# A hybrid GLA and RG-LRU layer on one core: the last modulation block on the vector engine, the gate row in a context bank

## The chip, the cores and the metric

The kernel runs on one core of a Trainium2 chip, in float32. The metric is the device time of one execution in microseconds (us). The engines are TensorE (PE; its weight loads are listed as PEld), VectorE (DVE), ScalarE (ACT), GpSimd (POOL) and SyncE (SP). Transfers that move data from and to HBM are issued by SP and by POOL.

## The reference

One layer with `D_MODEL` 2048, 512 latent tokens and 256 context tokens:

```python
mod_x = silu(c) @ w_ada + b_ada              # 3 x 2048: shift, scale, gate
mod_c = silu(c_ctx) @ w_ada + b_ada          # the same weights for the context
hn    = rmsnorm(h, g_norm) * (1 + scale) + shift
parts = split(hn @ w_in)                     # q, k, v, gates, recurrent input, merge gates
...                                          # gated linear attention and RG-LRU, both directions
x     = x + gate * merge_out(...)
out   = rmsnorm(x, g_final)
```

What matters here is the modulation: the products of two vectors (s = 0 for the latent tokens, s = 1 for the context) with the shift and scale columns of `w_ada`, 33.5 MB, and with its gate columns for s = 0 alone.

## The kernel before

Features stand on the partitions, in 16 groups of 128 called k. Every float32 operand of a large product is split into a rounded part (hi) and a rest (lo), ScalarE making hi and VectorE lo, and a product is three matmuls. The time from the beginning to about 206 us is written by `start` (L465). It has these streams of work:

- *Tokens.* Eight tiles `tok0` to `tok7` (two k each) are loaded, squared and summed for the norm; `tok8` to `tok11` (context) come later in the same way.
- *Modulation.* The shift and scale columns come as 64 pieces of 512 KB, cut into blocks (L43): blocks 0 to 3 hold one k and four pieces each, blocks 4 to 9 hold two k and eight pieces. `ada` (L676) multiplies the pieces of a block into PSUM tile `pa`, 32 rows wide (the two vectors and zeros), two pieces a call in blocks of two k. After the last piece of a block ScalarE copies `pa` out, `mod` (L701) transposes it into `pm` and builds the factors `AB`, and `modulate` (L725) makes xhi and xlo of each k: VectorE, ScalarE, VectorE (L731, L733, L735).
- *Key projection.* `key` (L832) works through a strict list (L748 to L754): first for every k the six column tiles of the latent keys (PSUM tiles `kx`), three items of two tiles for each k up to 13 and, for k = 14 and 15 together, six items of one tile and both k. An item is six matmuls of 512 columns. A second phase has the context keys (`kc`) and the two column tiles left over. The key weights come on POOL's queue as `kraw`, and `ksplit` (L783) splits them; those of k are asked for when those of k - 2 are split, and split when k - 3 is used up.

A planner in the code orders all this. It holds one clock per engine, an estimate of each transfer's landing (`fetch`, L481) and due times, and writes the instructions in the order in which its clocks reach them; on the chip each engine then runs its list in order. When key weights and the modulated k are ready it alternates between `ada` and key items. VectorE's and ScalarE's work stands in `todo` (done as soon as it is ready) and `idle` (when both engines have nothing planned).

Pieces land in buffers called slots: four tiles `araw0` to `araw3`, then `tok8` to `tok11` as long as they are not needed for the context (pieces from 24 on may not use them, L644), and from tok1 on each `tok` tile once both of its k are modulated (L742). `loads` (L640) issues the transfers in the fixed order `order` (L632) and stops at the first one for which no slot is free.

After the start the kernel runs a list of weight pieces through `run`. Side work is put between its matmuls: recurrent blocks (`rnn_block`, L983), whose products `rx` and `rc` use PSUM tags sa and sb with one bank each, and `gate_row` (L1073). The gate columns of the modulation are multiplied and added by VectorE into `gacc` (L1063 to L1067); for each half of the columns `gate_row` then sums over the partitions with two matmuls (L1079) into `pr`, tag sa, copies each row out (`grow`) and stores it. The tag pc has two banks, for the context accumulators of the projections that have any.

Of the kernel before, what the change touches and what calls it, by code (L numbers as in the profile page):

```python
# [5 lines left out]
F32 = mybir.dt.float32  # L6
F32R = mybir.dt.float32r
AF = mybir.ActivationFunctionType
ALU = mybir.AluOpType
# [3 lines left out]
P = 128  # L13
# [41 lines left out]
class Kern:  # L55
# [409 lines left out]
    def start(self, sp, raw0, raw, prime):  # L465
# [46 lines left out]
        hot = []  # L512
# [8 lines left out]
        def poll():  # L521
            n = 0
            while n < len(todo):
                if todo[n][0]() <= T["pe"]:
                    todo.pop(n)[1]()
                    n = 0
                else:
                    n += 1
            while max(T["dve"], T["act"]) <= T["pe"] + LAG:
                ok = [i for i in idle if i[0]() <= T["pe"]]  # L530
                if not ok:
                    break
                idle.remove(ok[0])
                ok[0][1]()
            loads()
# [90 lines left out]
        blocks = START_BLOCKS  # L626
        pieces = [(b, i) for b, ks in enumerate(blocks) for i in range(4 * len(ks))]

        slots = [(0.0, raw0.tile([P, 1024], F32, name=f"araw{i}")) for i in range(4)] + [(0.0, t) for t in tok[8:12]]
        araw = {}  # L630
        nada, nload = [0], [0]
        order = [("tok", i) for i in range(8)]  # L632
        for n in range(len(pieces)):
            order.append(("ada", n))
            if n in (3, 7):
                order.append(("key", 0))
            elif n in (31, 35, 39, 43):
                order.append(("tok", 8 + (n - 31) // 4))

        def loads():  # L640
            while nload[0] < len(order):
                kind, n = order[nload[0]]
                if kind == "ada":
                    f = [s for s in slots if n < 24 or all(s[1] is not t for t in tok[8:12])]  # L644
                    if not f:
                        return
                    slots.remove(f[0])
                    d, t = f[0]
                    araw[n] = t, fetch(t, a["wss"][n], dep=d)
                elif kind == "tok":  # L650
                    d = 0.0
                    if n >= 8:
                        f = [s for s in slots if s[1] is tok[n]]
                        if not f or px_done[0] < 2:
                            return
                        slots.remove(f[0])
                        d = f[0][0]
                    load_tok(n, d)
                else:
                    load_key(nc.sync)  # L660
                nload[0] += 1
# [2 lines left out]

        def ada_ready():
            n = nada[0]
            if n >= len(pieces):
                return INF
            b, i = pieces[n]

            w = n + len(blocks[b]) - 1
            if w not in araw:
                return INF
            return max(araw[w][1], pa_free[0] if i == 0 else 0.0)

        def ada():  # L676
# [18 lines left out]
            if i == 4 * m - 1:  # L695
# [2 lines left out]
                r = pa_free[0] = at("act", w / 1200 + 0.18, T["pe"] + 0.3)  # L698
                hot.append((lambda: max(r, sb_free[0]), lambda: mod(b, row, r)))

        def mod(b, row, r):  # L701
            m = len(blocks[b])
            pm = self.ps.tile([P, 2 * m, 4, 32], F32, tag="sb", name="pm")
            for j in range(2 * m):
                nc.tensor.transpose(pm[:, j, :, :].rearrange("p q c -> p (q c)"), row[:, j * P:(j + 1) * P], self.ident)
            t = pe("pm", 0.22 * m, r, sb_free[0])
            ms = sp.tile([P, 4, 4, 2], F32, tag="ms", name="ms")
            m4 = sp.tile([P, 4, 2, 2], F32, tag="m4", name="m4")
            m2 = sp.tile([P, 4, 2], F32, tag="m2", name="m2")
            v = nc.vector  # L710
            nc.scalar.activation(out=ms[:, 0:2 * m], in_=pm[:, :, :, 0:2], func=AF.Copy)
            t = sb_free[0] = at("act", 0.2, t + 0.2)
            v.tensor_tensor(out=m4[:, 0:2 * m], in0=ms[:, 0:2 * m, 0:2, :], in1=ms[:, 0:2 * m, 2:4, :], op=ALU.add)
            v.tensor_tensor(out=m2[:, 0:2 * m], in0=m4[:, 0:2 * m, 0, :], in1=m4[:, 0:2 * m, 1, :], op=ALU.add)
            for kk, k in enumerate(blocks[b]):
                v.tensor_scalar(out=AB[:, k, 0, :], in0=m2[:, kk, :], scalar1=sc1[:, k:k + 1],
                                scalar2=par[:, PC_GN + k:PC_GN + k + 1], op0=ALU.add, op1=ALU.mult)
                v.tensor_scalar(out=AB[:, k, 1, :], in0=m2[:, m + kk, :], scalar1=par[:, PC_SH + k:PC_SH + k + 1],
                                scalar2=None, op0=ALU.add)
            r = at("dve", 0.4 + 0.42 * m, t)  # L720
            for s in range(2):
                for k in blocks[b]:
                    (idle if s else todo).append((lambda s=s: max(r, tok_ok[s]), lambda k=k, s=s: modulate(k, s, r)))

        def modulate(k, s, r):  # L725
            hi, lo = ((self.xhi, self.xlo), (self.chi, self.clo))[s]
            w = width[s]
            n = 1024 // w
            x = tok[8 * s + k // n][:, k % n * w:k % n * w + w]
            m, b = AB[:, k, 0, s:s + 1], AB[:, k, 1, s:s + 1]  # L730
            nc.vector.scalar_tensor_tensor(out=x, in0=x, scalar=m, in1=rms[s], op0=ALU.mult, op1=ALU.mult)  # L731
            t = at("dve", w / 960 + 0.22, r, tok_ok[s])
            nc.scalar.activation(out=hi[:, k, :], in_=x, func=AF.Identity, bias=b)  # L733
            t = at("act", w / 1200 + 0.3, t)
            nc.vector.scalar_tensor_tensor(out=lo[:, k, :], in0=x, scalar=b, in1=hi[:, k, :].bitcast(F32), op0=ALU.add,  # L735
                                           op1=ALU.subtract)
            rk[k, s] = t = at("dve", w / 960 + 0.22, t)
            if s == 0:
                px_done[k // 2] += 1
                if px_done[k // 2] == 2 and k > 1:  # L740

                    slots.append((t, tok[k // 2]))  # L742
# [40 lines left out]
        def ksplit(n):  # L783
            t, r = kraw.pop(n)
            hi = self.ring.tile([P, 1024], F32R, tag="whi", name="khi")
            lo = self.ring.tile([P, 1024], F32R, tag="wlo", name="klo")
            w = cols[n // KT] // 2
            for u in (slice(0, w), slice(w, 2 * w)):
                nc.scalar.activation(out=hi[:, u], in_=t[:, u], func=AF.Copy)
                e = at("act", w / 1200 + 0.2, r)  # L790
                nc.vector.tensor_tensor(out=lo[:, u], in0=t[:, u], in1=hi[:, u].bitcast(F32), op=ALU.subtract)
                e = at("dve", w / 960 + 0.16, e)
            wk[n // KT, n % KT] = hi, lo, e
            kfree[n % 2] = e
            load_key(nc.gpsimd)
            ksplit_soon()
# [64 lines left out]

        loads()
        primed = None
        while nada[0] < len(pieces) or hot or fifo:
            poll()
            cand = []
            now = T["pe"]
            if hot:
                cand.append((hot[0][0](), 0))
            kr = key_ready()  # L870
            cand.append((kr, 2))

            if not (fifo and kr <= now and last[0] != "pa" and fifo[0][2][0] != ("x", 0)
                    and rk.get((fifo[0][1][-1] + 1, 0), INF) <= now):
                cand.append((ada_ready(), 1))
            t0 = max(now, min(c[0] for c in cand))
            pend = [t[0]() for t in todo] + [max(t[0](), T["dve"] - LAG, T["act"] - LAG) for t in idle]
            if t0 > now and pend and min(pend) < t0 and min(pend) > now:
                T["pe"] = min(pend)
                continue  # L880
            assert t0 < INF, (now, cand, pend, len(fifo))
            which = min((p for r, p in cand if r <= t0))
            if which == 0:
                hot.pop(0)[1]()
            elif which == 1:
                ada()
            else:
                key()
            if primed is None and nksplit[0] == 2 * KT and not kraw:
                primed = prime()  # L890
            if primed and len(fifo) <= 3:
                primed()
                primed = False
        for t in todo + idle:
            t[1]()

# [176 lines left out]
    def gate_row(self, acc, hf):  # L1073
        nc = self.nc
        for j in range(2):
            row = self.rp.tile([P, 512], F32, tag="grow", name="grow")[0:1]
            yield self.dep(acc)
            pr = self.ps.tile([1, 512], F32, tag="sa", name="pr")
            nc.tensor.matmul(pr, lhsT=self.ones, rhs=acc[:, j * 512:(j + 1) * 512], start=True, stop=True)  # L1079
            self.act(row, pr)  # L1080
            c0 = hf * 1024 + j * 512
# [623 lines left out]
```

## Time and profile before

| | us |
|---|---|
| median of 3 runs | 2301.71 (2299.45 to 2301.82) |
| the profiled execution | 2301.33 |
| its span | 2299.6 |
| PE, DVE, ACT, POOL busy | 2269.1, 1166.8, 1015.9, 104.6 |
| HBM read and written | 270.69 MB, 30.42 MB |

The span runs from the first to the last instruction; the time of the execution has a little more around it. Busy shares are means over the whole span. In rows, `128x512` is partitions by elements, `x8` a count of instructions. One float32 matmul of `ada`, `mod` and the sums shows as two matmul instructions, so one `ada` call of two pieces is `x8`.

### The profile page before, as it was taken

To read this page: it belongs to the slowest core of one execution; us is meant where nothing else is said; L and a number is where in the kernel's file an instruction comes from. 1 tells how busy PE (TensorE), PEld (TensorE's weight loads), DVE (VectorE), ACT (ScalarE), POOL (GpSimd) and SP (SyncE) were. 2 spreads that over 40 slices of the span, in tenths; PEclk is the share of its full clock that TensorE was granted. 3 is DMA by queue.
4 is the path that set the end of the run, shared out by engine and by line. 5 is a ranking of instruction groups with operands and counts; after the bars stand their busy time and mean duration, and the time that the engine had idled before them with its cause. 6 is when DMAs were issued, how large, how long until landed. Compare 5 with 4: busy or idle time off the path is not lost.

```text
span 2299.6 us, 29276 instructions
## 1 busy us (share of the span) xinstructions
PE 2269.1 (99%) x12032; PEld 1926.0 (84%) x12032; DVE 1166.8 (51%) x1498; ACT 1015.9 (44%) x1334; POOL 104.6 (5%) x201
## 2 busy tenths in 40 slices
PE   7999999999999999999999999999999999999998
PEld 4588889999898988998888888888888888888886
DVE  4563245655556655646637637637634423434435
ACT  3343255454454445546546556555523312222223
POOL 0010000000000000000000000000000000000000
PEclk9999999999999999999999999999999999999999
DMA  9943222333333332233233233323336633343533
GB/s 392 379 165 129 88 83 88 124 123 109 113 106 124 121 118 83 91 121 110 88 115 119 88 105 128 110 78 115 117 112 199 193 122 123 115 124 120 214 101 119
DMA packets 85814, 303.02 MB, mean 132 GB/s; under 512 B 10416, under 2 KB 11568, under 8 KB 84784
## 3 DMA queue, kind: packets, MB, share of 16 engines
q1 hardware_dynamic: 72656, 255.78, 33.1%
q0 software_dynamic: 13024, 45.37, 5.5%
q8 instruction: 94, 1.54, 0.3%
q14 instruction: 40, 0.33, 0.0%
HBM read 270.69 MB, written 30.42 MB: 131 GB/s over the span
## 4 chain that ended last, share of the span: by engine, by line
PE 85%; issue 10%; DMA 2%; ACT 1%; DVE 1%; POOL 0%; SPq 0%; DVEq 0%; POOLq 0%; ACTq 0%
PE px L127 64%; PE pc L127 6%; PE kx L850 4%; PE po L127 3%; PE kc L850 2%; PE rx L127 1%; PE pa L691 1%; PE pd L127 1%; DMA tok<-in_wss 1%; PE pcs L127 1%; PE rc L127 1%; PE pt L1450 0%; DMA tok<-in_xT 0%; POOL vS L936 0%; ACT g L90 0%
## 5 line engine op out<-in xcount | busy, mean ns | idle before, releaser
L94 DVE TENSOR_TENSOR wlo<-raw,whi 128x1024 fp32r<-128x1024 f32 x304 | 374.5, 1232 | 571.9 <-ACT whi L90 569.8
L90 ACT ACTIVATE whi<-raw 128x1024 fp32r<-128x1024 f32 x304 | 321.2, 1057 | 538.8 <-PE px L127 344.1
L127 PE MATMUL px<-xhi,whi 128*128 128x512 f32 x1408 | 551.0, 391 | 0.0
L127 PE MATMUL px<-xlo,whi 128*128 128x512 f32 x1408 | 549.3, 390 | 0.0
L127 PE MATMUL px<-xhi,wlo 128*128 128x512 f32 x1408 | 548.5, 390 | 0.0
L127 PEld LDWEIGHTS px<-xhi,wlo 128*128 128x128 f32 x1408 | 264.5, 188 | 55.6
L127 PEld LDWEIGHTS px<-xhi,whi 128*128 128x128 f32 x1408 | 264.8, 188 | 54.6 <-issue 2.6
L127 PEld LDWEIGHTS px<-xlo,whi 128*128 128x128 f32 x1408 | 264.9, 188 | 50.5
L127 PE MATMUL px<-whi,xlo 128*128 128x256 f32 x512 | 145.0, 283 | 0.0
L127 PE MATMUL px<-whi,xhi 128*128 128x256 f32 x512 | 145.0, 283 | 0.0
L127 PE MATMUL px<-wlo,xhi 128*128 128x256 f32 x512 | 145.0, 283 | 0.0
L90 ACT ACT_TABLE_LOAD x100 | 128.3, 1283 | 1.7
L127 PE MATMUL px<-yhi,whi 128*128 128x512 f32 x256 | 99.7, 389 | 0.0
L127 PE MATMUL px<-whi,mlo 128*128 128x512 f32 x256 | 99.7, 389 | 0.0
L127 PE MATMUL px<-yhi,wlo 128*128 128x512 f32 x256 | 99.7, 389 | 0.0
L127 PE MATMUL px<-olo,whi 128*128 128x512 f32 x256 | 99.7, 389 | 0.0
L127 PE MATMUL px<-ohi,whi 128*128 128x512 f32 x256 | 99.7, 389 | 0.0
L127 PE MATMUL px<-ohi,wlo 128*128 128x512 f32 x256 | 99.7, 389 | 0.0
L127 PE MATMUL px<-ylo,whi 128*128 128x512 f32 x256 | 99.7, 389 | 0.0
L127 PE MATMUL px<-whi,mhi 128*128 128x512 f32 x256 | 99.7, 389 | 0.0
L127 PE MATMUL px<-wlo,mhi 128*128 128x512 f32 x256 | 99.7, 389 | 0.0
L127 PEld LDWEIGHTS px<-wlo,xhi 128*128 128x128 f32 x512 | 98.3, 192 | 0.2
(328 smaller groups left out, 3966.0 us busy)
## 6 DMA issues: line engine op xcount, KB each, us to landing
raw<-in_w SPq DMA_DIRECT2D x304, 512.0 KB, 3.7
araw<-in_wss SPq DMA_DIRECT2D x35, 512.0 KB, 9.7
raw<-in_wgt SPq DMA_DIRECT2D x32, 512.0 KB, 4.3
tok<-in_wss SPq DMA_DIRECT2D x29, 512.0 KB, 9.7
kraw<-in_w POOLq DMA_DIRECT2D x16, 512.0 KB, 3.9
gS<-mst POOLq DMA_DIRECT2D x32, 256.0 KB, 2.5
gst<-gS POOLq DMA_DIRECT2D x32, 256.0 KB, 2.9
vS<-vt POOLq DMA_DIRECT2D x24, 256.0 KB, 2.5
```

Source lines behind the costliest of these rows:

```text
L90: return self.nc.scalar.activation(out=out, in_=in_, func=func, **kw)
L94: return self.nc.vector.tensor_tensor(out=out, in0=in0, in1=in1, op=op)
L127: self.nc.tensor.matmul(out, lhsT=lhsT, rhs=rhs, start=start, stop=stop, skip_group_check=True)
L691: nc.tensor.matmul(self.pa[32 * q:32 * q + 32], lhsT=S[:, k, :], rhs=raw_[:, kk * w:(kk + 1) * w], start=k < 4, stop=k >= KT - 4, skip_gro ...
L850: nc.tensor.matmul(o, lhsT=l[:, w], rhs=x[:, k, :], start=k == 0 and m == 0 and e == 0, stop=k == KT - 1 and m == 2, skip_group_check=True)
```

## The change

In `start`, the 64 pieces stay, but the last block's eight (56 to 63) are not multiplied by TensorE (`npe` is 56). They are loaded behind pieces 18, 22, ... 46. For each of them VectorE multiplies the two k-rows by the two vectors' columns and adds them into `vacc`, four instructions over 512 columns, 32 in all; they are written where the planner finds VectorE and ScalarE idle (`poll`) and between ScalarE's and VectorE's parts of a modulation or of a key split (`fill`). `vsum` then sums over the partitions with eight matmuls against ones and goes on with the factors as before (`factors`, taken out of `mod`). There are three `araw` tiles instead of four. In `gate_row`, `pr` gets a bank of tag pc instead of sa.

```diff
+                    if vq and vq[0][0] <= T["pe"]:
+                        vmul(*vq.pop(0))
+                        continue
...
+        npe = len(pieces) - 4 * len(blocks[-1])
+        vacc = raw0.tile([P, 2, 512], F32, name="vacc")
+        vq = []
+        def fill():
+            if vq and vq[0][0] <= T["dve"]:
+                vmul(*vq.pop(0))
-        slots = [(0.0, raw0.tile([P, 1024], F32, name=f"araw{i}")) for i in range(4)] + [(0.0, t) for t in tok[8:12]]
+        slots = [(0.0, raw0.tile([P, 1024], F32, name=f"araw{i}")) for i in range(3)] + [(0.0, t) for t in tok[8:12]]
-        for n in range(len(pieces)):
+        for n in range(npe):
             order.append(("ada", n))
...
+            if n >= 18 and n % 4 == 2 and npe + (n - 18) // 4 < len(pieces):
+                order.append(("ada", npe + (n - 18) // 4))
...
+        def vmul(r, n, t, kk, s):
+            k = 2 * pieces[n][1] + kk
+            x, o, c = t[:, kk * 512:(kk + 1) * 512], vacc[:, s, :], self.cs[:, s, k:k + 1]
+            if k == 0:
+                nc.vector.tensor_scalar(out=o, in0=x, scalar1=c, scalar2=None, op0=ALU.mult)
+            else:
+                nc.vector.scalar_tensor_tensor(out=o, in0=x, scalar=c, in1=o, op0=ALU.mult, op1=ALU.add)
+            e = at("dve", 0.75, r)
+            if kk and s:
+                slots.append((e, t))
+            voff[0] += 1
+            if voff[0] == 32:
+                hot.append((lambda: max(e, sb_free[0]), lambda: vsum(e)))
+        def vsum(r):
+            b = len(blocks) - 1
+            pm = self.ps.tile([P, 4, 2, 2], F32, tag="sb", name="pm")
+            for j in range(4):
+                for s in range(2):
+                    nc.tensor.matmul(pm[:, j, s, :], lhsT=vacc[:, s, j * P:(j + 1) * P], rhs=ones[:, 0:2],
+                                     start=True, stop=True)
+            t = pe("pm", 2.4, r, sb_free[0])
+            m2 = sp.tile([P, 4, 2], F32, tag="m2", name="m2")
+            nc.scalar.activation(out=m2, in_=pm[:, :, :, 0], func=AF.Copy)
+            t = sb_free[0] = at("act", 0.2, t + 0.2)
+            factors(b, m2, t)
...
             nc.scalar.activation(out=hi[:, k, :], in_=x, func=AF.Identity, bias=b)
+            fill()
...
                 nc.scalar.activation(out=hi[:, u], in_=t[:, u], func=AF.Copy)
+                fill()
...
-            pr = self.ps.tile([1, 512], F32, tag="sa", name="pr")
+            pr = self.pc.tile([P, 512], F32, tag="pc", name="pr")[0:1]
```

## Rows read from the trace of the kernel before

**Rows 1.** The page: busy time by engine, and the chain that ended last, by line.

```profile
...
PE 2269.1 (99%) x12032; PEld 1926.0 (84%) x12032; DVE 1166.8 (51%) x1498; ACT 1015.9 (44%) x1334; POOL 104.6 (5%) x201
...
PE px L127 64%; PE pc L127 6%; PE kx L850 4%; PE po L127 3%; PE kc L850 2%; PE rx L127 1%; PE pa L691 1%; PE pd L127 1%; DMA tok<-in_wss 1%; PE pcs L127 1%; PE rc L127 1%; PE pt L1450 0%; DMA tok<-in_xT 0%; POOL vS L936 0%; ACT g L90 0%
...
```

**Rows 2.** Stretches: length, busy of PE, PEld, DVE, ACT, POOL, PE clock, DMA share, GB/s.

```profile
...
45.00:60.00 15.00, 15.00 (x85) 7.81 (x88) 5.86 (x17) 3.73 (x9) 1.08 (x2) 1.00 0.93 370
60.00:72.00 12.00, 12.00 (x64) 7.35 (x56) 4.13 (x7) 3.70 (x9) 1.07 (x2) 1.00 0.86 314
72.00:119.80 47.80, 44.83 (x237) 23.31 (x237) 28.17 (x71) 18.10 (x39) 3.22 (x6) 1.00 1.02 411
119.80:140.26 20.46, 20.46 (x96) 15.99 (x95) 13.64 (x29) 11.19 (x23) 1.59 (x3) 1.00 0.37 114
140.26:206.00 65.74, 65.74 (x467) 61.92 (x466) 26.80 (x47) 22.91 (x42) 7.40 (x15) 1.00 0.43 139
...
```

**Rows 3.** PE's waits, 29 to 140 us: us in total, times, longest.

```profile
...
PE pa L691 <- DMA araw<-in_wss: 3.0, 5, 1.2
PE pa L691 <- DMA tok<-in_wss: 1.0, 2, 0.8
...
```

**Rows 4.** The chain of waits in the start: start us, us, what.

```profile
...
18.42 1.80 PE pr L585 x8
...
101.54 0.58 PE pr L594 x4
...
105.47 2.74 PE kx L850 x12
...
116.54 2.92 PE pa L691 x24
...
123.41 1.59 PE kx L850 x6
124.99 0.44 PE pm L705 x4
...
```

**Rows 5.** DVE in order of time: start us, us, what [idle before].

```profile
...
76.18 0.75 DVE L735 SCALAR_TENSOR_TENSOR xlo<-tok,AB,xhi 128x512 fp32r<-128x512 f32 x1 [0.79 <-ACT xhi L733]
76.85 0.74 DVE L731 SCALAR_TENSOR_TENSOR tok<-tok,AB,rms 128x512 f32<-128x512 f32 x1
...
92.10 0.75 DVE L735 SCALAR_TENSOR_TENSOR xlo<-tok,AB,xhi 128x512 fp32r<-128x512 f32 x1 [0.79 <-ACT xhi L733]
...
```

**Rows 6.** DVE's groups, 360 to 900 us: busy us, mean ns.

```profile
...
L99 DVE TENSOR_SCALAR gacc<-raw,cs 128x1024 f32<-128x1024 f32 x2 | 1.5, 748 | 0.0
```

**Rows 7.** SP's issues in order of time, and SP's waits, 45 to 72 us.

```profile
...
49.61 9.44 SPq L482 DMA_DIRECT2D araw<-in_wss  x4
63.13 0.33 SPq L482 DMA_DIRECT2D tok<-in_wss  x1
...
SPq L482 <- PE pa L691: 10.3, 3, 3.8
SPq L482 <- DVE xlo L735: 6.1, 2, 4.0
...
```

**Rows 8.** Key weight loads (POOL's queue): issue to landing.

```profile
...
DMA to landing us min/median/max: 3.7/6.0/9.9
```

**Rows 9.** PE in order of time, two instructions.

```profile
...
85.20 0.62 PE L691 MATMUL pa<-tok,S 128*32 128x512 f32 x2
...
140.26 0.28 PE L850 MATMUL kc<-chi,khi 128*128 128x256 f32 x1
...
```

**Rows 10.** All engines in order of time, around the gate rows.

```profile
...
620.61 0.59 ACT L90 ACTIVATE grow<-pr 1x512 f32<-1x512 f32 x1 [3.26 <-DMA rS<-grow]
...
621.25 0.50 PE L127 MATMUL rx<-xh,wh 128*128 128x512 f32 x1 [0.38 <-ACT grow L90]
...
886.12 1.02 PE L1079 MATMUL pr<-gacc,ones 128*1 128x512 f32 x2 [0.79 <-ACT grow L90]
...
```

More of the change, by code (lines that the diff above doesn't have):

```diff
@@ L627, in start @@
         pieces = [(b, i) for b, ks in enumerate(blocks) for i in range(4 * len(ks))]
-        slots = [(0.0, raw0.tile([P, 1024], F32, name=f"araw{i}")) for i in range(4)] + [(0.0, t) for t in tok[8:12]]
+        npe = len(pieces) - 4 * len(blocks[-1])
+        vacc = raw0.tile([P, 2, 512], F32, name="vacc")
+        voff = [0]
+        vq = []
[3 more added lines that the diff above has]
+        slots = [(0.0, raw0.tile([P, 1024], F32, name=f"araw{i}")) for i in range(3)] + [(0.0, t) for t in tok[8:12]]
         araw = {}
@@ L648, in loads @@
                     d, t = f[0]
-                    araw[n] = t, fetch(t, a["wss"][n], dep=d)
+                    r = fetch(t, a["wss"][n], dep=d)
+                    if n < npe:
+                        araw[n] = t, r
+                    else:
+                        for kk in range(2):
+                            for s in range(2):
+                                vq.append((r, n, t, kk, s))
                 elif kind == "tok":
@@ L666, in ada_ready @@
             n = nada[0]
-            if n >= len(pieces):
+            if n >= npe:
                 return INF
@@ L699, in ada @@
                 hot.append((lambda: max(r, sb_free[0]), lambda: mod(b, row, r)))
+        def vmul(r, n, t, kk, s):
[3 more added lines that the diff above has]
+                nc.vector.tensor_scalar(out=o, in0=x, scalar1=c, scalar2=None, op0=ALU.mult)
+            else:
+                nc.vector.scalar_tensor_tensor(out=o, in0=x, scalar=c, in1=o, op0=ALU.mult, op1=ALU.add)
[9 more added lines that the diff above has]
+            for j in range(4):
+                for s in range(2):
+                    nc.tensor.matmul(pm[:, j, s, :], lhsT=vacc[:, s, j * P:(j + 1) * P], rhs=ones[:, 0:2],
[5 more added lines that the diff above has]
+            factors(b, m2, t)
         def mod(b, row, r):
@@ L714, in mod, with factors @@
             v.tensor_tensor(out=m2[:, 0:2 * m], in0=m4[:, 0:2 * m, 0, :], in1=m4[:, 0:2 * m, 1, :], op=ALU.add)
+            at("dve", 0.4, t)
+            factors(b, m2, t)
+        def factors(b, m2, t):
+            m, v = len(blocks[b]), nc.vector
             for kk, k in enumerate(blocks[b]):
@@ L719, in mod @@
                                 scalar2=None, op0=ALU.add)
-            r = at("dve", 0.4 + 0.42 * m, t)
+            r = at("dve", 0.42 * m, t)
             for s in range(2):
@@ L863, in start @@
         primed = None
-        while nada[0] < len(pieces) or hot or fifo:
+        while nada[0] < npe or hot or fifo:
             poll()
@@ L876, in start @@
             t0 = max(now, min(c[0] for c in cand))
-            pend = [t[0]() for t in todo] + [max(t[0](), T["dve"] - LAG, T["act"] - LAG) for t in idle]
+            pend = [t[0]() for t in todo] + [max(v[0], T["dve"] - LAG, T["act"] - LAG) for v in vq[0:1]] + [max(t[0](), T["dve"] - LAG, T["act"] - LAG) for t in idle]
             if t0 > now and pend and min(pend) < t0 and min(pend) > now:
@@ L893, in start @@
                 primed = False
+        assert not vq
         for t in todo + idle:
```

## The prediction

> **What bounds the kernel now.** I read the page first. TensorE is busy 99% of the span and one group of projection matmuls makes up 64% of the chain that ended last [rows 1], so a gain must be TensorE work taken away or a TensorE wait removed. Both edits lie in short stretches. The first is the start, up to the la pieces at about 206 us; I cut it into stretches next [rows 2]. TensorE is packed from 45 to 72 us and from 119.8 us on, and has its gaps in between: 47.80 - 44.83 = 3.0 us from 72 to 119.8. The column of bytes shows a second resource at its limit. The DMA engines move 411 GB/s from 72 to 119.8 and next to none of the start's operands after that, so the last piece of w_ada lands at about L = 119.8 us. Between 45 and 72 they move 370 and 314 GB/s: against 411 that is 15 x 41/411 + 12 x 97/411 = 1.5 + 2.8 = 4.3 us of idle transfer time. The list of waits names what TensorE lacks: pieces of w_ada, 4.0 us in seven waits [rows 3]. So from 72 to 119.8 TensorE (3.0 us short of full) and the transfers (full) are both within a few per cent of being the bound, and that decides what an edit here is worth.
>
> **The change, part by part.**
>
> *TensorE work of the last block.* Block 9 (k = 14, 15; pieces 56 to 63) costs four calls of `ada`. Three of them back to back took 2.92 us [rows 4], so four take 3.9 us. A key item after a call takes 1.59 instead of 2.74/2 = 1.37 us, 0.22 us for each of the two places where calls and items alternate, 0.4 us in all. The four transposes take 0.44 us. Sum removed: 4.7 us. Added: `vsum` with eight matmuls of two columns against a 128x128 operand. Two such took 0.58 us at 101.5 us [rows 4], so eight take 2.3 us; four took 1.80 us at 18.4 us, which gives 3.6 us as the other end. The block ends late, near the first row's time, so I take 2.3. TensorE loses 2.4 us of work (1.1 to 2.4).
>
> *VectorE work.* 32 instructions over 512 columns. 30 have the form of the modulation's own scalar_tensor_tensor, 0.75 us long and 0.67 us from start to start [rows 5]: 20 us. Two are tensor_scalar; one over 1024 columns took 748 ns [rows 6], so 0.4 us each. Together 21 us, set among 5.9 + 4.1 + 28.2 = 38 us of VectorE work in the 75 us from 45 to 119.8 [rows 2], so it fits. `fill` puts one where VectorE waits 0.79 us for ScalarE in the middle of a modulation [rows 5]: 0.67 into 0.79 costs nothing. In a split of key weights the wait is shorter and up to 0.5 us is lost, but those are made up to two k ahead. If a piece lands later than planned, VectorE waits in order with the modulation's second half behind it: 0 to 1.2 us a time, the largest of seven by which TensorE's own pieces came late [rows 3]. I take 0 and keep the cost for the rival.
>
> *Transfers.* Not a byte less is moved. Eight pieces of 0.524 MB, 1.28 us each at 411 GB/s, are put between pieces 18 and 47, so every block from 4 to 8 comes later by the pieces put ahead of it, and the last to land is now block 8 (k = 12, 13). In the old order it was block 9. All else that had landed by L must also land by the new last piece L', except perhaps one load of key weights (0.39 MB, 0.96 us): these are asked for as TensorE uses up earlier k, and TensorE will be later with them; I take off 0.5 us. Hence L' = 119.8 + (i - 4.3) - 0.5, with i the idle transfer time of the new order. Using some of the 4.3 us is the one real gain here.
>
> What is i? The old idle time comes from landing buffers. From 49.6 to 59.05 SP issues only four pieces and the next comes at 63.1, while SP stands waiting for `ada` calls and for modulations to free a buffer [rows 7]. The code says which: pieces from 24 on may not use tok8 to tok11, so they have araw0 to araw3 and tok1. After the change a buffer fewer is there (vacc takes its room), pieces 56 to 63 fall under the same rule from piece 18 on, and each holds its buffer until four VectorE instructions (2.7 us, after a wait for gaps that I put at 2.5) are through. For it, SP has more to issue in that time, and may: piece 56 goes out before 24. A transfer takes at least 3.7 us from issue to landing [rows 8]; with half a piece (0.64 us) of waiting for its pair, one call (1.0 us) and half a key item (0.7 us) a buffer is held 6.0 us, one of VectorE some 9 us, about 6.6 us on the mean. One piece per 1.28 us, beside a key-weight load every four pieces (0.24 us a piece), needs 6.6/1.52 = 4.3 buffers. Four are there until k = 4 and 5 are done near 63 us, five until about 80. So the gap shrinks little: i from 0 (all used) to 8 (nearly twice as much); I take 3.5, near the old row, and L' = 118.5 us.
>
> The Trainium skill ("DMA: Bandwidth & Descriptors", "Anatomy of one DMA — SWDGE (gpsimd) path") gives a transfer some 2.0 us fixed plus its bytes at 436 GB/s, which would be 3.2 us here, below the shortest measured landing of 3.7; by it the need would be 4.0 buffers and i perhaps 3.0, an estimate that moves the end by 0.5 us. The same page's "Specifications" put the limit of HBM for one core at about 358 GB/s; the 411 GB/s of this trace [rows 2] shows that it doesn't bind here, so I give no weight to a stream slower than before.
>
> *From the last landing to the end of the first key phase.* Block 6's last `ada` call began at 85.20 us [rows 9] and its first k was modulated at 92.10 + 0.75 = 92.85 [rows 5]: 7.65 us by row, transposes and VectorE, including one key item. I take 7.5. Behind it now stand four k, 12 key items of 1.37 us: 16.4 us. Before, only k = 14 and 15 stood behind the last landing: 7.5 + 8.2 = 15.7 us, ending at 135.5, so that chain had 4.8 us to spare before the phase really ended, at 140.26 us [rows 9]. Now it is 23.9 us: 118.5 + 23.9 = 142.4 us. TensorE's own work gives only 140.26 - 2.4 = 137.9, so it is late data, not work, that sets the end: TensorE does 2.4 us less and stands idle 4.5 us more. From 140 to 206 us TensorE is 100% busy [rows 2], and there is no gap in which to give the shift back. Start: +2.1 us.
>
> *Gate row.* `pr` shares bank sa with the recurrent blocks. TensorE waited 0.79 us for the bank at the second of a pair of row matmuls and 0.38 us at a recurrent block [rows 10]. In a context bank a row's predecessor has been read out long before: -1.2 us at most, 0 if the next context product meets the unread second row. That row's copy waits 3.26 us for the store of the first [rows 10], but the code has at least one other context tile between. I take -1.2.
>
> Sum: +2.1 - 1.2 = +0.9 us on the profiled execution's own 2301.33 us, 1.7 us more than its span: 2302.2 us. The median shown, 2301.71, is 0.4 above that execution.
>
> **Rivals.**
> A. *TensorE is the bound, late data or not.* For it: 100% from 119.8 on. Then the phase ends 2.4 us earlier and with the late pieces gone also the 3.0 us of gaps go: -2.4 to -5.4, with the gate row 2297.7 to 2294.7. Against it: L' would have to be 137.9 - 23.9 = 114.0 or less, and even i = 0 gives 115.0.
> B. *Buffers held by VectorE starve the transfers* (slower). Place: 46 to 80 us. Each further microsecond of i moves L', and with it the end, by one. With i = 8, L' = 123.0 and the phase ends at 146.9: +6.6 - 1.2 = +5.4, 2306.7 us. A late piece that stops VectorE ahead of a modulation adds up to 1.2 us more. It is slower than before from L' = 117.6 (140.26 + 1.2 - 23.9), that is i = 2.6, and slower by 0.2% from i = 7.2. For it: SP's waits and the buffer count above. Against it: TensorE takes pieces at once when it starves, which frees buffers sooner than in the old order.
> C. *It doesn't do what it says*: the multiplications find no gaps and collect behind block 8's modulations. Unfinished ones, at worst the last two pieces with 8 x 0.67 = 5.4 us, would hold k = 12: 2302.2 + 5.4 = 2307.6. Against it: 37 us of free VectorE time before L.
>
> **How the numbers follow.** 0.2% is 4.6 us, about what a measurement of this kernel can tell from no change: 2297.1 to 2306.3 counts as the same. The forecast (i from 1 to 6: 2299.8 to 2304.8) gets 0.6, A 0.15, B 0.19, C 0.06. Half of A lies beyond -0.2%, and I add 0.04 for an order that helps where I saw none: faster 0.12. Of B some two thirds pass +0.2%, and all of C: slower 0.2. The same: 0.68. The range reaches to the middle of A and just past B and C: 2296.5 to 2308.
>
> **What would show it.** Right: the stream at 411 GB/s stops near 118 us with block 8's pieces last; TensorE's gaps between 50 and 125 us grow from 3 to about 7 us, before the first key items of k = 6, 8, 10 and 12; the first `kc` matmul starts at about 142; no wait stands at the `pr` and `rx` matmuls of the gate row. Wrong: the first `kc` matmul before 139, or gaps that do not grow (A); a long hole in the transfers between 50 and 80 us (B); vacc instructions still running when block 8 is modulated, or waiting for a transfer (C).

## The result, and the profile after

The changed kernel takes 2313.58 us (median of 4 runs, 2311.15 to 2314.78), the kernel before in the same comparison 2301.77 (2299.45 to 2302.4): ratio 1.0051, 95% interval 1.0038 to 1.0063. It is slower by 12 us where I forecast no change; 2313.58 lies outside the range of 2296.5 to 2308. The profiled execution took 2313.61 us, its span is 2311.9.

Lines of the page that answer to [rows 1], and stretches that answer to [rows 2] (same columns):

```profile
PE 2274.9 (98%) x12012; PEld 1927.6 (83%) x12012; DVE 1187.3 (51%) x1528; ACT 1015.8 (44%) x1333; POOL 104.6 (5%) x201
...
PE px L127 72%; PE pc L127 8%; PE kx L906 3%; PE po L127 3%; PE kc L906 2%; PE rx L127 2%; PE pd L127 1%; PE pa L712 1%; PE rc L127 1%; PE pcs L127 1%; DMA tok<-in_wss 1%; DMA araw<-in_wss 1%; DMA tok<-in_xT 0%; PE pt L1508 0%; ACT xres L90 0%
```

```profile
45.00:60.00 15.00, 13.80 (x74) 6.88 (x73) 10.10 (x25) 3.58 (x8) 1.58 (x3) 1.00 0.92 343
60.00:72.00 12.00, 11.09 (x49) 6.12 (x50) 6.54 (x11) 2.38 (x4) 0.54 (x1) 1.00 0.86 313
72.00:119.80 47.80, 40.34 (x185) 19.78 (x185) 32.09 (x66) 15.08 (x30) 2.65 (x5) 0.96 0.97 374
119.80:140.26 20.46, 18.48 (x91) 11.93 (x86) 13.85 (x35) 7.25 (x16) 0.04 (x1) 1.00 0.24 92
140.26:206.00 65.74, 65.74 (x430) 60.25 (x429) 33.13 (x62) 28.07 (x53) 9.53 (x19) 1.00 0.49 158
```

From 140 us on TensorE is packed as before, so the whole loss is made ahead of that. The context's first key matmul, which answers to the second of [rows 9], shows how large it is:

```profile
153.81 0.28 PE L906 MATMUL kc<-chi,khi 128*128 128x256 f32 x1
```

153.81 - 140.26 = 13.55 us later; the gate rows give some of it back (below). The list of PE's waits, 28 to 160 us, answers to [rows 3]:

```profile
PE pa L712 <- DMA araw<-in_wss: 3.8, 5, 1.2
PE pa L712 <- DMA tok<-in_wss: 3.2, 4, 2.2
PE pm L754 <- ACT row L718: 2.2, 3, 0.7
PE kx L906 <- ACT xhi L787: 2.0, 3, 1.1
PE kx L906 <- DVE xlo L790: 0.9, 3, 0.3
```

Seven waits of 4.0 us for pieces have become nine of 7.0, and TensorE also waits for modulated rows (`xhi`, `xlo`), which the same list of the kernel before does not have. Up to the first `kc`, TensorE was busy 123.28 us before and is busy 129.22 now, though four calls were taken from it, and idle 24.6 us instead of 17.0. PE in order of time shows where both grow:

```profile
99.85 1.05 PE L712 MATMUL pa<-araw,S 128*32 128x512 f32 x4 [1.16 <-DMA araw<-in_wss]
103.08 1.59 PE L712 MATMUL pa<-tok,S 128*32 128x512 f32 x4 [2.18 <-DMA tok<-in_wss]
104.60 0.79 PE L906 MATMUL kx<-xhi,khi 128*128 128x512 f32 x1
105.19 0.63 PE L906 MATMUL kx<-xlo,khi 128*128 128x512 f32 x1
...
117.32 1.06 PE L712 MATMUL pa<-tok,S 128*32 128x512 f32 x8
...
120.89 1.05 PE L712 MATMUL pa<-tok,S 128*32 128x512 f32 x4 [0.23 <-DMA tok<-in_wss]
122.92 1.05 PE L712 MATMUL pa<-araw,S 128*32 128x512 f32 x4 [0.97 <-DMA araw<-in_wss]
```

A single piece (`x4`) takes 1.05 us and a pair (`x8`) 1.06: where TensorE has caught up with the transfers, a call falls apart into halves, and each half lasts as long as a whole call. From 28 us to the first `kc` all `pa` matmuls together take 36.95 us for 56 pieces; before they took 33.16 for 64.

SP's waits, 45 to 130 us, name who holds the landing buffers; `vacc`, VectorE's sums, is new among them:

```profile
SPq L482 <- PE pa L712: 22.6, 17, 3.8
SPq L482 <- DVE xlo L790: 16.0, 4, 5.8
SPq L482 <- DVE vacc L728: 14.9, 6, 5.5
```

The two longest of these, 5.8 us for a modulation and 5.5 us for `vacc`, follow one another from 98.7 to 112 us, and with them the stream has its largest hole after 72 us (108 to 116 us: 267 and 286 GB/s where [rows 2] have 411):

```profile
108.00:112.00 4.00, 4.00 (x21) 2.36 (x21) 2.06 (x4) 0.94 (x2) 0.00 (x0) 1.00 0.68 267
112.00:116.00 4.00, 4.00 (x24) 2.68 (x23) 2.24 (x10) 0.80 (x2) 0.54 (x1) 1.00 0.80 286
```

The last pieces land at about 124.6 us (the stretch 124 to 125 moves 248 GB/s, the next 31). PE's groups from there to the first `kc` show what was still to be done (busy us, mean ns | idle before):

```profile
L906 PE MATMUL kx<-xhi,khi 128*128 128x512 f32 x36 | 14.3, 398 | 0.5 <-ACT xhi L787 0.5
...
L712 PE MATMUL pa<-tok,S 128*32 128x512 f32 x8 | 1.6, 605 | 0.0
L742 PE MATMUL pm<-ones,vacc 128*128 128x2 f32 x12 | 1.5, 251 | 0.0
L754 PE MATMUL pm<-ident,row 128*128 128x128 f32 x4 | 0.6, 272 | 0.0
```

36 matmuls with xhi and khi are 18 key items, all those of k = 10 to 15. Behind the last landing of the kernel before (119.8 us) there were 28, 14 items.

The gate row did what was forecast: from 260 us on no wait stands at `pr` or `rx`; before there were 0.8 and 0.4 us.

### The profile page after: what moved, and what is told of

Read it like the earlier page. It is cut to its first block, busy times and chain, and to the rows that moved or that the text cites. A ratio compares the mean times of both kernels' runs of the same rounds, so it can differ in the third digit from the quotient of the medians.

```text
span 2311.9 us, 29252 instructions
## 1 busy us (share of the span) xinstructions
PE 2274.9 (98%) x12012; PEld 1927.6 (83%) x12012; DVE 1187.3 (51%) x1528; ACT 1015.8 (44%) x1333; POOL 104.6 (5%) x201
## 4 chain that ended last, share of the span: by engine, by line
PE 95%; DMA 2%; ACT 1%; DVE 1%; issue 0%; SPq 0%; DVEq 0%; ACTq 0%
PE px L127 72%; PE pc L127 8%; PE kx L906 3%; PE po L127 3%; PE kc L906 2%; PE rx L127 2%; PE pd L127 1%; PE pa L712 1%; PE rc L127 1%; PE pcs L127 1%; DMA tok<-in_wss 1%; DMA araw<-in_wss 1%; DMA tok<-in_xT 0%; PE pt L1508 0%; ACT xres L90 0%
```

## The experiments

Each ran beside the kernel before (2300.7 to 2301.8 us), so the ratio and its interval are what is compared. "First kc" and "pa" (TensorE's time with pieces from 28 us to the first `kc`) come from one execution, the profiled one; for e3 it was the slowest of four (2316.68 us).

| run | us | ratio, 95% interval | first kc | pa |
|---|---|---|---|---|
| before | 2301.77 | | 140.26 | 33.16 |
| after | 2313.58 | 1.0051 (1.0038 to 1.0063) | 153.81 | 36.95 |
| e1 gate row alone | 2299.27 | 0.9994 (0.9984 to 1.0003) | 139.46 | 32.90 |
| e2 last block alone | 2315.25 | 1.0062 (1.0047 to 1.0077) | 153.38 | 35.34 |
| e3 11 of 32 multiplications | 2311.80 | 1.0053 (1.0038 to 1.0068) | 156.84 | 37.05 |
| e4 pieces late | 2330.03 | 1.0129 (1.0112 to 1.0146) | 169.03 | 33.45 |
| e5 pieces not loaded | 2300.38 | 0.9998 (0.9989 to 1.0007) | 141.23 | 32.03 |
| e6 before, three buffers | 2312.15 | 1.0048 (1.0031 to 1.0065) | 149.81 | 35.35 |
| e7 pieces early | 2310.78 | 1.0042 (1.0027 to 1.0057) | 149.17 | 34.25 |
| e8 k = 12 first | 2314.66 | 1.0060 (1.0045 to 1.0075) | 152.44 | 37.20 |
| e9 four buffers | 2311.12 | 1.0042 (1.0029 to 1.0054) | 150.35 | 35.27 |
| e10 five buffers, no VectorE | 2297.98 | 0.9988 (0.9979 to 0.9997) | 138.93 | 35.11 |
| e11 e9, pieces early | 2313.04 | 1.0051 (1.0038 to 1.0064) | 154.56 | 34.23 |
| e12 e9, 11 multiplications | 2310.26 | 1.0041 (1.0029 to 1.0054) | 152.15 | 34.18 |
| e13 e9, not loaded | 2297.95 | 0.9989 (0.9980 to 0.9997) | 137.39 | 28.97 |
| e14 e12, pieces late | 2319.18 | 1.0078 (1.0065 to 1.0092) | 159.66 | 32.58 |
| e15 e9, unread | 2327.01 | 1.0109 (1.0092 to 1.0126) | 168.47 | 41.75 |
| e16 own place, unread | 2305.49 | 1.0019 (1.0011 to 1.0028) | 146.11 | 33.84 |
| e17 own place, all work | 2305.55 | 1.0024 (1.0014 to 1.0033) | 144.62 | 32.53 |
| e18 later piece first | 2321.80 | 1.0092 (1.0079 to 1.0106) | 158.73 | 30.11 |

**Which edit (e1, e2).** e1 is the kernel before with this one line, e2 the changed kernel without it.

```diff
-            pr = self.ps.tile([1, 512], F32, tag="sa", name="pr")
+            pr = self.pc.tile([P, 512], F32, tag="pc", name="pr")[0:1]
```

> The kernel before with the gate row's bank alone changed. My prediction's term: the 0.79 and 0.38 us waits go, 1.2 us less than before, about 2300.6 us. Rival: the row's matmuls only move and nothing is gained, 2301.8 us; if the bank collides with the context accumulators, more than 2302.5.

> The changed kernel with the gate row back in its old bank, so the last block on VectorE alone. If the loss lies in the start, as the later first kc matmul says (153.8 against 140.3 us): 13.0 us above before, 2314.8 us. If part of it came from the gate row's bank: less than 2312.

e2 has the whole loss. e1's interval holds the 1.2 us forecast and no change as well.

**VectorE's work (e3).**

```diff
-            if k == 0:
+            if n == npe:
...
-            else:
+            elif kk and s:
```

> The changed kernel, but VectorE issues 8 of the 32 multiplications (one per piece, the one that frees its buffer; the last block's sums are left incomplete). Place in the stream (the eight pieces delay blocks 4 to 8): nearly the loss of the changed kernel, 10 us or more above before. Work on VectorE (32 instructions ahead of modulations and a buffer held until they are through): most of the loss goes, under 5 us above before.

11 multiplications are left (not 8 as expected above), four for the first piece and one for each other. The loss stays, so VectorE's time isn't the price. What this run can't say is whether the order, still written for 32, is.

**The place of the pieces (e4, e7).** e4 loads them behind pieces 41, 43, ... 55, e7 behind 8, 10, ... 22 (and lets them use `tok8` to `tok11`).

```diff
-            if n >= 18 and n % 4 == 2 and npe + (n - 18) // 4 < len(pieces):
-                order.append(("ada", npe + (n - 18) // 4))
+            if n >= 40 and n % 2 == 1:
+                order.append(("ada", npe + (n - 41) // 2))
```

```diff
+            if n >= 8 and n % 2 == 0 and npe + (n - 8) // 2 < len(pieces):
+                order.append(("ada", npe + (n - 8) // 2))
...
```

> The changed kernel with the eight pieces loaded behind pieces 41, 43, ... 55 instead of 18, 22, ... 46. Place in the stream: blocks 4 to 7 come as early as before, the loss falls by more than half, under 6 us above before. VectorE or one buffer less: the 32 instructions are pressed together ahead of blocks 8 and 9 and the buffer is still missing, so 10 us or more above before.

> The changed kernel with the eight pieces loaded behind pieces 8, 10, ... 22 instead of 18, 22, ... 46, and allowed into tok8 to tok11. Buffers in the stretch from 46 to 72 us as the main price: a loss of 5 to 8 us above before instead of 13, since the pieces then lie where eight buffers can be used. Eight transfers ahead of the blocks as the main price, wherever they stand: 11 us or more above before.

e4 shows rival C's mechanism: 10.9 us of waits of TensorE for ScalarE's rows behind multiplications that run to 149 us, and 1.29% instead of 0.51%. Not all of that is waiting: up to the first `kc` TensorE is busy 135.20 us, 6.0 more than in the changed kernel, at a mean granted clock of 0.92 (0.99 there). e7's 9.7 us of loss lie between its two expectations, and it gains nothing that can be told from the changed kernel; TensorE is busy 21.61 of 27 us from 45 to 72 us (24.89 in the changed kernel): what it spares at the end it starves for here.

**A buffer, or the pieces (e5, e6).** e5 is the changed kernel without the eight loads and what hangs on them (first diff), e6 the kernel before with one number changed (second).

```diff
+        nc.gpsimd.memset(vacc, 0.01)
...
-            if n >= 18 and n % 4 == 2 and npe + (n - 18) // 4 < len(pieces):
-                order.append(("ada", npe + (n - 18) // 4))
...
```

```diff
-        slots = [(0.0, raw0.tile([P, 1024], F32, name=f"araw{i}")) for i in range(4)] + [(0.0, t) for t in tok[8:12]]
+        slots = [(0.0, raw0.tile([P, 1024], F32, name=f"araw{i}")) for i in range(3)] + [(0.0, t) for t in tok[8:12]]
```

> The changed kernel without the eight pieces: they are neither loaded nor multiplied (the last block's sums are a constant), the sums over partitions come behind block 8, and there are still three araw buffers. Late data through eight pieces ahead of blocks 4 to 8: without them TensorE has 2.4 us less work and nothing to wait for, the first kc matmul near 138 us, 2298 us. One buffer fewer as the cause: most of the loss stays, 2308 us or more.

> The kernel before with three araw buffers instead of four, nothing else. If the missing buffer starves the transfers by itself: 4 us or more above before, 2305 us. If it is the eight extra pieces that need the buffers: within 2 us of before.

Without the pieces, three buffers can't be told from the kernel before (e5, 0.9998). But a buffer fewer alone makes the kernel before slower by 1.0048, as much as the whole change (e6). e6's stretches from 72 us:

```profile
72.00:119.80 47.80, 43.71 (x222) 23.65 (x222) 26.44 (x68) 17.74 (x36) 2.69 (x5) 0.96 0.99 373
```

Its stream ends at about 124.5 us (124 to 125: 191 GB/s, then 37), like that of the changed kernel. I took the missing buffer for the answer; e9 shows that it was not.

**The order of the last keys (e8).** `vsum` is written behind block 8's factors, so that k = 12 is modulated ahead of 14.

```diff
-                hot.append((lambda: max(e, sb_free[0]), lambda: vsum(e)))
+                held.append(e)
...
+            if b == len(blocks) - 2:
+                e = held[0]
+                hot.append((lambda: max(e, sb_free[0]), lambda: vsum(e)))
```

> The changed kernel with vsum only behind block 8's factors, so that k = 12 and 13 are modulated ahead of 14 and 15. In the changed kernel 14 and 15 went first and TensorE waited 2.0 us for k = 12. If that order is part of the loss: 2 to 3.5 us faster than the changed kernel, 2310 us. If TensorE has other work all that time: the same, 2313 us.

No gain, so that order is no part of the loss that can be told.

**The buffer given back (e9 to e11).** Room for a fourth `araw` beside `vacc` comes from two edits, kept in e9 to e17. They were not run by themselves; e10 and e13, which have them, are both faster than the kernel before.

```diff
-            g = sp.tile([P, 512], F32, tag="hf", name="diag", bufs=2)
+            g = rms[s]
...
-                row = sp.tile([P, 512], F32, tag="hf", name="row", bufs=2)
+                row = sp.tile([P, 512], F32, tag="hf", name="row", bufs=1)
```

> The changed kernel with its fourth landing buffer given back beside the sums (room for it is made by writing the diagonal matrices into the rms tiles and keeping one row tile instead of two). Theory (the missing landing buffer starves the transfers): the stream is again idle for about 3.5 us instead of 9.8, the first context key matmul comes at 140 to 146 us and the time is 2300 to 2306 us. Rival (it is the detour over VectorE itself, pieces held there and its sums collected late): the first context key matmul stays at 150 us or later and the time at 2310 us or above. If both take part, between 2306 and 2310.

> The kernel before with the gate row in a context bank and five landing buffers instead of four, all blocks on TensorE (rms tiles and row tile as in e9). Theory (transfers idle for want of a buffer, in the kernel before too): the idle time falls from 3.5 towards 1 us, the first context key matmul comes at 137 to 139 us, and the time is 2296 to 2299 us. Rival (at four buffers TensorE's own order sets the pace, a fifth does nothing): first context key matmul at 139 to 141 us, 2299 to 2301 us as in e1.

> e9 with VectorE's eight pieces loaded earlier, behind pieces 8, 10, ... 22, as in e7. Theory (buffer): VectorE's sums are complete long before the end and the last block's keys come from TensorE's floor; 2298 to 2304 us, no later than e9. Rival (pieces that TensorE needs come 8 transfers later from the outset, so TensorE waits there whatever the buffers are): 45 to 72 us shows TensorE under 23 of 27 us busy, as in e7 (21.6), and the time is 2306 us or above.

My theory fell with e9: the stream ended at about 118.6 us (118 to 119: 248 GB/s, then 33), nearly where I had forecast it, and yet the first `kc` came at 150.35. PE's groups from 118.7 us on:

```profile
L906 PE MATMUL kx<-xhi,khi 128*128 128x512 f32 x36 | 14.4, 399 | 0.6 <-ACT xhi L787 0.6
...
L712 PE MATMUL pa<-araw,S 128*32 128x512 f32 x8 | 2.1, 604 | 1.3 <-DMA araw<-in_wss 1.3
L742 PE MATMUL pm<-ones,vacc 128*128 128x2 f32 x16 | 1.9, 253 | 0.0
```

Again 18 key items were left. e11 repeats e7: 8.51 of 12 us busy from 60 to 72 us. e10 is e1 with these edits and `range(5)`. It shows the other direction, the stream fuller with a fifth buffer and all blocks on TensorE: 395 and 358 GB/s where [rows 2] have 370 and 314, and hardly a gap of TensorE from 72 us on.

```profile
45.00:60.00 15.00, 13.83 (x70) 6.94 (x69) 4.56 (x13) 3.03 (x7) 1.07 (x2) 1.00 1.00 395
60.00:72.00 12.00, 12.00 (x70) 6.98 (x68) 6.02 (x15) 4.33 (x9) 1.07 (x2) 1.00 0.97 358
72.00:119.80 47.80, 47.49 (x246) 24.94 (x241) 27.99 (x66) 18.52 (x36) 3.23 (x6) 1.00 0.99 396
```

e10 is faster than both kernels, though its interval overlaps e1's.

**The transfers, the work or the held buffers (e12 to e15).** All have four buffers. e12 writes the order for 11 multiplications, e13 leaves the eight pieces out, e14 is e12 with e4's places, and e15 puts this in place of the four entries of a piece:

```diff
+                        slots.append((r, t))
...
```

> e9 with 11 of the 32 multiplications (four for the first piece, one for each other), the order of the work written for that: all eight pieces are still loaded at their places, their buffers come free after one multiplication, the sums are incomplete. Theory (eight transfers of 1.27 us, 10 us, stand ahead of TensorE's pieces in a stream that is at its limit and give it no work meanwhile): first context key matmul at 147 us or later, 2307 to 2312 us. Rival (VectorE's 21 us of work hold buffers and modulations up): first context key matmul at 138 to 143 us, 2298 to 2303 us.

> e9 without the eight transfers and without the multiplications; the sums of the last block hold a constant. Theory (the transfers' place): TensorE's pieces land up to 10 us earlier than in e12 and the first context key matmul is at 136 to 139 us, 2295 to 2299 us; the difference e12 to e13 is 9 us or more. Rival (VectorE's work): e12 and e13 within 4 us of one another.

> e12 with its eight pieces loaded behind pieces 41, 43, ... 55 instead of 18, 22, ... 46 (11 of the 32 multiplications as there). Theory (place): TensorE's pieces of blocks 3 to 6 land earlier, TensorE is busy over 14 of 15 us in 45 to 60 and 11.5 of 12 in 60 to 72, and with next to nothing for VectorE to collect the loss is mostly gone: first context key matmul at 138 to 144 us, 2298 to 2304 us. Rival (eight transfers without work for TensorE cost the same wherever they stand): within 2 us of e12, 2307 us or above.

> e9 with its eight pieces loaded at their places and read by nobody, so that each buffer is free as soon as its piece has landed; the sums of the last block hold a constant. Theory (eight transfers of 1.27 us ahead of TensorE's pieces): first context key matmul at 146 us or later, 2306 to 2311 us. Rival (buffers held until VectorE is through): first context key matmul at 137 to 142 us as in e13, 2297 to 2302 us.

e12 against e13 settles that the work isn't it: 12.3 us lie between them, and 21 fewer multiplications (e9 to e12) give 0.9. In e13 TensorE's 56 pieces take 28.97 us, what I had reckoned (33.16 less 3.9 and 0.4); its stretch from 28 us to the first `kc`, `pa` alone (PE busy, clock, DMA share, GB/s):

```profile
28.00:137.39 109.39, 28.97 (x236) 1.00 0.80 312
```

e14 went the way of neither theory. Until 72 us it is as the place theory said, 15.00 of 15 and 12.00 of 12 us, and then the sums come late: its eight pieces are multiplied 6.3 to 9.9 us apart, the last at 140.19, and TensorE waits 8.9 us for ScalarE's rows. From the code I take it that `fill` writes one entry of the queue between two rows, four entries a piece, also where an entry has no work; that was not tried by itself. e15 decides nothing. A buffer that is free on paper is taken at once, and SP, which issues in order, stands until the piece in it has landed:

```profile
SPq L482 <- DMA araw<-in_wss: 47.6, 6, 9.0
SPq L482 <- DMA tok<-in_wss: 13.4, 2, 7.2
```

**No landing buffer touched (e16, e17).** The eight pieces land where the context's parts will stand, in memory that nothing uses until then, at their old places in the stream; e16 has no entries in `vq`, and e17's `vmul` no longer appends to `slots`. In both the context's own modulations are held back until those pieces are through.

```diff
+                if kind == "ada" and n >= npe:
+                    j = n - npe
+                    t = self.sink[j % 2][:, j // 2, :]
+                    r = fetch(t, a["wss"][n])
...
```

> Four landing buffers for TensorE as in e9; the eight pieces land at their old places in the stream, but in the memory of the context's parts, and nobody reads them; the sums of the last block hold a constant. Theory (eight transfers of 1.27 us ahead of TensorE's pieces in a full stream): first context key matmul at 145 to 150 us, 2304 to 2310 us. Rival (landing buffers held by VectorE): as in e13, 137 to 142 us and 2297 to 2302 us.

> e16 with all 32 multiplications, so that the whole block is computed by VectorE and holds no landing buffer. Theory (place of the transfers): within 3 us of e16, 2304 to 2311 us. Rival (VectorE's work, through modulations that come later): 4 us or more above e16.

Both are as the place theory had them, and alike in time (1.0019 and 1.0024), but not in how they come to it. e16's stream nearly stops from 112 to 115 us. SP waits 11.0 us, up to 114.9, for a modulation to free a `tok` tile, TensorE waits 1.3 us for a row of ScalarE's, and the last pieces land at about 120 us. One stretch, and one line of SP's waits, 45 to 130 us:

```profile
114.00:116.00 2.00, 1.32 (x11) 0.49 (x12) 1.41 (x3) 1.72 (x5) 0.00 (x0) 1.00 0.09 14
SPq L483 <- DVE xlo L794: 21.8, 4, 11.0
```

e17's stream has no such hole and ends at about 115. So e16 is not the transfers alone, and the two don't show that 32 multiplications cost nothing in these places. e17's stretches and its groups from the last landing (114 to 115: 270 GB/s, then 31) to the first `kc`:

```profile
45.00:60.00 15.00, 14.98 (x78) 7.98 (x76) 10.38 (x26) 3.28 (x7) 1.62 (x3) 1.00 1.02 415
60.00:72.00 12.00, 10.53 (x50) 5.93 (x50) 9.29 (x16) 2.38 (x4) 0.54 (x1) 1.00 1.01 408
72.00:119.80 47.80, 43.08 (x225) 23.02 (x218) 34.49 (x77) 16.90 (x35) 2.69 (x5) 0.96 0.91 367
```

```profile
L910 PE MATMUL kx<-xhi,khi 128*128 128x512 f32 x36 | 14.3, 398 | 0.6 <-ACT xhi L791 0.6
...
L742 PE MATMUL pm<-ones,vacc 128*128 128x2 f32 x16 | 1.9, 252 | 0.0
L714 PE MATMUL pa<-tok,S 128*32 128x512 f32 x4 | 1.1, 604 | 0.2 <-DMA tok<-in_wss 0.2
```

The stream has no hole left from 45 to 72 us (415 and 408 GB/s), and still TensorE has 1.5 us of gaps from 60 to 72 and 18 items behind the last landing.

**Half calls (e18).** The changed kernel with a call's pieces in reverse order.

```diff
-            for _ in range(m):
...
+            for u in reversed(range(m)):
...
```

> The changed kernel, but each ada call multiplies its later piece first, so that it waits once and the pair's matmuls run together. Theory 1 (single pieces are a cost of their own): TensorE's pa time falls from 36.95 towards 30 us, idle time grows by less than half of that, the first context key matmul comes at 147 to 150 us and the time is 2306 to 2310 us. Theory 2 (the long pa time is waiting for pieces in another form): pa time falls likewise, but the idle time grows by as much, the first context key matmul stays at 151 to 156 us and the time at 2311 to 2316 us.

PE's waits of e18, 28 to 170 us:

```profile
PE pa L709 <- DMA tok<-in_wss: 7.1, 4, 2.7
PE pa L709 <- DMA araw<-in_wss: 6.9, 5, 2.7
```

`pa` falls by 6.8 us and idle time grows from 24.6 to 30.7, by 6.1: so far the second theory, by which a half call is waiting in another form. That the first `kc` comes later than in the changed kernel (158.73 us), and the kernel is slower than it, was in neither theory, so e18 doesn't show it cleanly. TensorE's other work up to there takes 5.7 us more, at a mean clock of 0.92 instead of 0.99 (0.75 over 119.8 to 140.26 us, 1.00 in the changed kernel). SP waits 28.3 us for `pa` instead of 22.6; the code has the earlier piece of a pair hold its buffer until the later has landed.

**The ladder.** With four buffers, one step each: without the pieces 0.9989 (e13), with their transfers 1.0019 (e16), with the work too 1.0024 (e17), with landing buffers held for it 1.0042 (e9), with one buffer fewer 1.0051 (the change). The eight transfers at these places, with VectorE's work, cost 0.0035 (e13 to e17); that the work has no part in it rests on e9 and e12 (1.0042 and 1.0041 with 21 multiplications fewer), since e16 has a hole of its own. The held buffers cost 0.0018 (half-widths 0.0010 and 0.0013, together 0.0016, so just told from zero). On top of the rest, the missing buffer's 0.0009 can't be told from zero, though alone it costs 0.0048. I take it that both act by the same means, TensorE's pieces coming later; the runs fit that and don't single it out.

e13 also shows how little there was to gain: with the last block's pieces and work gone altogether (and the gate row's new bank), the kernel is 0.0011 faster than before. e10, with the gate row's new bank and a fifth buffer and no work moved, is 0.0012 faster.

## Why the prediction was wrong

The step that failed is the chain from the last landing to the end of the first key phase, 7.5 + 16.4 = 23.9 us, and with it the idle transfer time i = 3.5; the changed kernel shows 29.2 and 9.6. Term by term:

*Idle transfer time.* Forecast 3.5 (bounds 0 to 8), which gave L' = 118.5. The stretches give 15 x 68/411 + 12 x 98/411 + 47.8 x 37/411 = 9.6 us, and L' is 124.6: 6.1 us of the miss. This is rival B's mechanism, past its bound of 8 and mostly out of its place: from 45 to 72 us the idle time is 5.3 us, only 1.0 more than before, and 4.3 us lie behind that, where the stream had been full, 2.6 of them from 108 to 116 us. I had looked for holes up to 72 us, and up to 80 in B. My count of buffers held the right things, but a mean of 6.6 us a buffer said nothing of a queue in which one late buffer stops all that follow.

*The formula L' = 119.8 + (i - 4.3) - 0.5* held: with i = 0 it gives 115.0, and e17, with no hole up to 72 us, ends at 115; with i = 9.6, counted up to 119.8 us, it gives 124.6, as measured (some 0.5 us more of idle time lies between the two, as much as the 0.5 taken off for a load of key weights, which no run shows). With e9's fourth buffer the stream ended at 118.6, where I had put it.

*Behind the last landing.* Forecast 23.9, measured 29.2 in the changed kernel, 31.7 in e9, 29.6 in e17: 5.3 us of the miss, and together with L' all of it (153.8 - 142.4 = 11.4). I took 7.5 us from block 6, where one key item stood in it, and let TensorE's other work vanish in it. Here the six items of k = 10 and 11 (6 x 1.37 = 8.2 us), the sums (1.5), transposes (0.6) and calls (1.6) are 11.9 us, and gaps 0.8. The text held the warning: before, that chain ended 4.8 us ahead of the real end, so TensorE's work and not latency was the longer of the two. I should have counted the work left to TensorE at L', as for e17: 18 items of 1.37 us, 24.7, and 4.2 of other work make 28.9; measured 29.6.

Why more work is left is the mechanism that I had priced at nothing. That every block from 4 to 8 comes later by the pieces put ahead of it stands in the prediction, but I followed it only to the last landing. In a full stream a piece for VectorE takes 1.28 us in which nothing lands that TensorE can use, and what it buys, the keys of k = 14 and 15, can't start until the whole block is summed. So TensorE runs dry in the middle and has 18 key items to do at the end, where I had counted 12 and the kernel before had 14. e17 against e13 prices it with no landing buffer held by VectorE: 7.6 us.

*TensorE's work.* Forecast -2.4 us; up to the first `kc` TensorE was busy 5.9 us more. The four calls are saved (e13: 28.97 us for 56 pieces), and `vsum` took 1.9 (forecast 2.3); but the 56 pieces took 8.0 us more as half calls and at the lower clock. How the 8.0 divide between the two is not shown; e18 fits most of it being waiting, so late data again. The Trainium skill ("TensorE: Matmul & The Clock Gate", "Part 3: Packing small matmuls — row/col tiling") says that matmuls in different column tiles of the array run at the same time; the trace agrees, with 1.05 us for a piece (two of the four column tiles `32 * q`) and 1.06 for a pair (all four).

*VectorE.* 32 instructions at 743 and 479 ns, and TensorE never waits for them, as forecast; DVE waits 2.5 us for their pieces. They cost through the buffers that they hold: SP waits 14.9 us for `vacc`. Rival C is not what happened here, but e4 and e14 show how near it lies. *Rival A*'s floor of 137.9 us was near: e13 reaches 137.39, once the transfers are gone. *The gate row*'s waits went as forecast.

*The chances.* The forecast's own mechanism, late data, was the right one, and B its right form; both I bounded by transfers alone, and gave 8 us as the most that i could be.

## What to carry to other kernels

Where a transfer stream is full, as here, moving work to an idle engine need not free the bound one: ask what each landing lets the bound engine do, and count the work that is left for it when the last one lands, item by item. A landing buffer taken or held can cost as much, so price it by a run of the old kernel with one buffer fewer before counting what the buffer is used for. Loads that the bound engine doesn't need did better in memory of their own (e17 against e9); whether they would cost nothing in the stream's holes was not tried.

## What the runs showed of the hardware

TensorE's clock fell within this stage. The changed kernel's stretches (columns as in [rows 2]):

```profile
101.00:102.00 1.00, 0.00 (x0) 0.00 (x0) 0.95 (x3) 0.72 (x1) 0.00 (x0) 1.00 1.06 436
102.00:103.00 1.00, 0.00 (x0) 0.00 (x0) 1.00 (x2) 0.00 (x0) 0.00 (x0) 1.00 0.99 408
103.00:104.00 1.00, 0.92 (x4) 0.14 (x4) 0.99 (x2) 0.64 (x1) 0.00 (x0) 0.73 1.01 410
104.00:105.00 1.00, 1.00 (x3) 0.40 (x2) 0.75 (x1) 0.45 (x2) 0.00 (x0) 0.50 1.02 414
105.00:106.00 1.00, 1.00 (x3) 0.76 (x3) 0.69 (x1) 0.26 (x1) 0.00 (x0) 0.50 1.04 418
106.00:107.00 1.00, 1.00 (x4) 0.76 (x3) 0.32 (x1) 0.63 (x1) 0.00 (x0) 0.56 1.03 410
107.00:108.00 1.00, 1.00 (x6) 0.82 (x5) 0.97 (x3) 0.00 (x0) 0.00 (x0) 1.00 1.06 397
```

TensorE stood from 100.9 to 103.08 us, and then worked at 0.50 (1.2 GHz) for some 3 us: a half call took 1.59 us instead of 1.05, a key matmul 0.63 instead of 0.39. Ahead of it it had stood 1.16 us more (before 99.85). The kernel before shows 1.00 in every stretch of [rows 2]; e6 shows the same fall from 79 to 82 us, behind a wait of 1.8. From 103 to 107 us the clock's loss is 0.27 + 0.50 + 0.50 + 0.44 = 1.7 us: a wait of 2.2 us cost nearly twice itself, which no term of mine had. In other runs the clock matters more: the mean clock up to the first `kc` is 1.00 in the kernel before, e9, e13 and e16, 0.99 in the changed kernel and e17, 0.96 in e2, whose start is the changed kernel's, and 0.92 in e4 and e18. So the steps of the ladder were profiled at nearly one clock, while a part of e4's and e18's loss is the clock.
